# A streaming-encoder trunk on one core: odd tiles of frames normed and turned by a matrix product on TensorE, projected in pairs

## The chip, the cores and the metric

The kernel runs on one core of a Trainium2 chip. Its engines work beside each other, each through its own instructions in order: TensorE (PE, matrix products into the banks of PSUM), VectorE (DVE), ScalarE (ACT), GpSimd (POOL) and SyncE (SP), whose work here is to issue DMAs; ScalarE and GpSimd issue some too. Semaphores make one engine wait for another. The time is that of one execution on the device, in microseconds (us); of several executions the median counts.

## The reference

Batch 1, 2048 frames of 1024 channels, 16 learned frames ("meta tokens") ahead of them, depth 1. So the layer is an S5 mixer and a gated convolutional FFN, each behind an RMS norm and with a residual:

```python
hn = rms_norm(h, norm_mix)                       # h: meta tokens and x, 2064 x 1024
u = (hn @ s5_w_in).reshape(bsz, L, 64, 16)       # 64 groups of 16 channels
bu = einsum('gph,blgh->blgp', b_bar, u)          # complex, 64 states a group
s = scan(s[t] = a_bar * s[t - 1] + bu[t])        # complex, diagonal, over the frames
y = gelu(re(c s) + d_skip * u)
a, g = split(y @ s5_w_glu); h = h + a * sigmoid(g)
hn = rms_norm(h, norm_ffn)
h = h + (silu(conv(hn @ up_a)) * conv(hn @ up_b)) @ w_down
return h[:, 16:]
```

`a_bar` and `b_bar` come from `lam_re`, `lam_im`, `log_dt` and `b_re`, `b_im` (exponential, sine, cosine). All is float32.

## The kernel before

Matrix products with the large weights are made of three fp16 products (`mm3`, lines 76 to 78: high by high, high by low, low by high), so every operand is split into a high and a low fp16 part.

The first stage, which the change touches, projects the normed frames by `s5_w_in`. The 2048 frames are held as 16 tiles (`r` = 0 to 15) of 128 frames; a tile takes every sixteenth frame, and tile `r` holds frame 15 - r of each group of 16. The meta tokens are a tile of their own, `r = T = 16`. The order of the tiles is `seq` = 0, 1, 16, 2, 3, ... 15. A tile goes through these steps:

- `load_x` (L165): the tile, 512 KB, from HBM into a slot that the later stages will use for something else.
- `norm_a` (L171): sum of squares on ScalarE, then `rstd_of` on GpSimd (L70, L72).
- `norm_b` (L177, L178, L180): high part on ScalarE, low part on VectorE, both into `hl`, which has two slots that take turns; then two DMA transposes on SP's queue put them into `hnT[0]` and `hnT[1]`, with channels on the partitions.
- `emit_u(cb, q, part, w)` (L382): block `cb` of 128 channels of `u`, quad `q` (four tiles); `part` and `w` choose tiles in the quad. Eight steps of 128 input channels, three products each. The result fills a bank of PSUM.
- `evict_u` (L392): GpSimd puts a column of the meta tokens' result into `us` (L404), ScalarE the rest (L405), SP stores it to the DRAM tensor `ud` (L406). `load_u` (L412) reads it back as `U`, with another layout.

In this stage the blocks 0 to 2 are projected; their weights are loaded by `load_win`, scaled by the norm's gains and split by `split_win` (L352, L355, L357 for blocks 1 and 2; L354, L355, L357 for block 3). The blocks 3 to 7 follow in the next stage, the loop over `p`.

Beside it, `params()` is a generator whose steps (`next(par)`) compute `a_bar`, its powers `pre` and `pim` and the scan's coefficients `asc`: small operations on VectorE, `pow` on GpSimd (L245), a few transposes on TensorE. From them come the first block's matrices: `gen_b(0)` (L435 to L455, VectorE) and `transp(0)` (L465, L467) make `Win`, which turns `U` into states; `transp_c` (L473 to L476) and `gen_c(0)` (L487 to L493, VectorE) make `CA`, which turns states into outputs. `load_bc(0)` (L422, L425) loads their inputs in seven DMAs. `zero_kd` (L206, L208) and `load_cst` (L621) are small preparations for later stages.

The order is written out by hand: what a loop body emits, an engine runs in that order. `plan` says what is projected and evicted after which tile, `psteps` how many parameter steps are taken; quad 0 is projected tile by tile, quad 1 in halves, quads 2 and 3 whole. After the last tile come the rest of the quads, `transp_c`, `gen_b`, `drive(par)`, `gen_c`, `load_u(0)`, `transp(0)` and block 3's weights, mixed as `plan[15]` lists them. Then follow `emit_v(0)` (L534, L537: states from `Win` and `U`), `tcv` (L699) and its copies (L700, L701), and the loop over `p`, in which VectorE makes the next block's matrices and scans the states.

Of the kernel before, what the change touches and what calls it, by code (L numbers as in the profile page):

```python
# [11 lines left out]
F32 = mybir.dt.float32  # L12
# [3 lines left out]
P = 128  # L16
# [28 lines left out]
def tile_kernel(ctx: ExitStack, tc: tile.TileContext, x, meta, norm_mix, norm_ffn, w_in, lam_re, lam_im, log_dt,  # L45
# [95 lines left out]
    with ExitStack() as c2:  # L141
# [10 lines left out]
        def load_x(r, eng):  # L152

            if r == T:
                xt = s5.tile([P, D], F32, tag="tmp", name="xm")
            elif r < 3 or r >= 13:
                tag, bufs = (("S", 2), ("S", 2), ("Z", 1))[r if r < 3 else r - 13]
                xt = s5.tile([P, D], F32, tag=tag, bufs=bufs, name=f"xt{r}")
            else:
                if r % 2:  # L160
                    tag, bufs = (("Win", 1), ("CA", 2), ("CA", 2), ("U", 2), ("U", 2))[(r - 3) // 2]
                    xslots[r // 2] = s5.tile([P, 2, D], F32, tag=tag, bufs=bufs, name=f"xs{r}")
                xt = xslots[(r - 1) // 2 if r % 2 == 0 else r // 2][:, 1 - r % 2]
            n = P if r < T else T
            eng.dma_start(out=xt[:n], in_=x3[T - 1 - r] if r < T else meta)  # L165
            return xt

        def norm_a(r, xt):
            n = P if r < T else T
            ss = ld.tile([P, 1], F32, tag="ss", bufs=4, name=f"ss{r}")  # L170
            A.activation(junk[:n], xt[:n], AF.Square, accum_out=ss[:n])  # L171
            return rstd_of(ld, ss, n, f"a{r}")

        def norm_b(r, xt, rs):
            n = P if r < T else T
            hi, lo = hl[:n, r % 2, 0], hl[:n, r % 2, 1]
            A.activation(hi, xt[:n], AF.Copy, scale=rs[:n])  # L177
            V.scalar_tensor_tensor(lo, xt[:n], rs[:n], hi, op0=ALU.mult, op1=ALU.subtract)  # L178
            for t, s in zip(hnT if r < T else hmT, (hi, lo)):
                SY.dma_start_transpose(out=t[:, :, r, :] if r < T else t, in_=s)  # L180
# [21 lines left out]
            V.tensor_copy(gains[:, 8:16], tg[:, 8:16])  # L202

        def zero_kd():
            zero = ld.tile([P, 7 * T], F32, tag="zero", bufs=1, name="zero")
            V.memset(zero, 0.0)  # L206
            for i in range(2):
                SY.dma_start(out=kd[i].rearrange("h g x -> (h g) x")[:, 0:7 * T], in_=zero)  # L208
# [123 lines left out]
        def load_win(cb):  # L332
            if 0 < cb < 3:
                st = s5.tile([P, DK, P], F32, tag="wit", bufs=2, name=f"wst{cb}")
            else:
                st = ld.tile([P, DK, P], F32, tag="wst", bufs=1, name=f"wst{cb}")
            SY.dma_start(out=st, in_=wv[:, :, cb * P:(cb + 1) * P])
            return st

        def split_win(cb, st):  # L340
            wp = ld.tile([P, 2, DK, 16, 8], F16, tag="win", bufs=3, name=f"win{cb}")
            ws = [wp[:, i] for i in range(2)]
            src = st.rearrange("p dk (g h) -> p dk h g", h=16)
            if cb == 0:
                for dk in range(DK):
                    A.activation(ws[0][:, dk], src[:, dk], AF.Copy, scale=gains[:, dk:dk + 1])
                    V.scalar_tensor_tensor(ws[1][:, dk], src[:, dk], gains[:, dk:dk + 1], ws[0][:, dk], op0=ALU.mult,
                                           op1=ALU.subtract)
            else:
                for dk in range(DK):  # L350
                    if cb in (1, 2):
                        V.tensor_scalar(st[:, dk], st[:, dk], gains[:, dk:dk + 1], None, op0=ALU.mult)  # L352
                    else:
                        A.activation(st[:, dk], st[:, dk], AF.Copy, scale=gains[:, dk:dk + 1])  # L354
                A.copy(ws[0], src)  # L355
                yield
                V.tensor_tensor(ws[1], src, ws[0], op=ALU.subtract)  # L357
            yield
            wt[cb] = [t.rearrange("p dk h g -> p dk (h g)") for t in ws]
# [22 lines left out]
        def emit_u(cb, q, part=None, w=1, tag=0, dks=range(DK)):  # L382
            wh, wl = wt[cb]
            if (cb, q) not in ups:
                ups[cb, q] = psum.tile([P, 4, P], F32, tag=utags[tag], name=f"u{cb}_{q}")
            ps = ups[cb, q]
            r = slice(0, 4) if part is None else slice(part, part + w)
            rr = slice(4 * q + r.start, 4 * q + r.stop)
            for dk in dks:
                mm3(ps[:, r], wh[:, dk], wl[:, dk], hnT[0][:, dk, rr], hnT[1][:, dk, rr], dk == 0, dk == DK - 1)  # L390
# [26 lines left out]
        def load_bc(cb, eng=PO):  # L417
            gs = slice(G * cb, G * cb + G)
            xs = s5.tile([P, 2, G, T], F32, tag="X", name=f"X_{cb}")
            for i in range(2):  # L420
                for c, b in enumerate((b_re, b_im) if i == 0 else (b_im, b_re)):
                    eng.dma_start(out=xs[64 * c:64 * c + 64, i], in_=b[0, gs].rearrange("g p h -> p g h"))  # L422
            ct = s5.tile([P, 3, 64], F32, tag="ct", name=f"ct{cb}")
            for i, cc in enumerate((c_re, c_im, c_re)):
                eng.dma_start(out=ct[:, i], in_=cc[0, gs].rearrange("g h p -> (g h) p"))  # L425
            return xs, ct
# [182 lines left out]
        def drive(*gens):  # L609
            gens = list(gens)  # L610
            while gens:
                for g in list(gens):
                    if next(g, 0) == 0:
                        gens.remove(g)
# [15 lines left out]
        for r in seq[1:3]:  # L630
# [3 lines left out]
        ws[2] = load_win(2)  # L634
        xt[3] = load_x(3, SY)
        next(par)
        na[0] = norm_a(0, xt[0])
        setup(gst)
        plan = {0: "s", 1: "s", 2: "s", 3: "su", 5: ("h04", "h14", "h24"), 7: ("h06", "h16", "h26"), 8: ("e00", "e10"),
                9: ("e20",), 11: ("m022", "m123"), 12: ("e01", "e11", "e21", "m220"), 13: ("w",),  # L640
                14: (), 15: ("m031", "k", "b", "p", "c", "e02", "e12", "e22", "e03", "l", "m132", "t", "m233",
                              "x", "e13", "e23")}
        psteps = {**{i: 1 for i in range(0, 11)}, 11: 1, 12: 2, 13: 1, 14: 1, 15: 1, 16: 1}
        for i, r in enumerate(seq):
            if i == 0:
                norm_b(r, xt.pop(r), na.pop(r))
                drive(split_win(0, ws.pop(0)))
            for r2 in seq[i + 2:i + 3] if i else seq[1:3]:
                na[r2] = norm_a(r2, xt[r2])
            if i:  # L650
                norm_b(r, xt.pop(r), na.pop(r))
            if i + 5 < len(seq):
                xt[seq[i + 5]] = load_x(seq[i + 5], A)
            if 0 < i < 3:
                drive(split_win(i, ws.pop(i)))
            if r == 5:
                bc = load_bc(0, SY)
            if r == 6:
                zero_kd()
                load_cst()  # L660
            for _ in range(psteps.get(i, 0)):
                next(par, 0)
            for e in plan.get(r, ()):
                if e == "s":
                    for cb in range(min(3, r + 1)):
                        for part in range(r + 1) if r == cb else (r,):
                            emit_u(cb, 0, part=part, tag=cb)
                elif e == "u":
                    emit_u_meta([0, 1, 2])
                elif e[0] == "h":  # L670
                    for part in (int(e[2]) % 4,):
                        emit_u(int(e[1]), 1, part=part, w=2, tag=(3, 4, 0)[int(e[1])])
                elif e == "p":
                    drive(par)
                elif e == "b":
                    drive(gen_b(0, bc[0]))
                elif e == "k":
                    transp_c(0, bc[1])
                elif e == "c":
                    drive(gen_c(0))  # L680
                elif e == "t":
                    transp(0)
                elif e == "w":
                    ws[3] = load_win(3)
                elif e == "x":
                    drive(split_win(3, ws.pop(3)))
                elif e == "l":
                    load_u(0)
                elif e[0] == "m":
                    emit_u(int(e[1]), int(e[2]), tag=int(e[3]))  # L690
                else:
                    evict_u(int(e[1]), int(e[2]))
        quads = [(cb, q) for cb in range(3, NCB) for q in range(4)]
        takes = [3, 3, 3, 3, 4, 4, 0, 0]
        wn = 4
# [758 lines left out]
```

## Time and profile before

| | us |
|---|---|
| median of 3 executions | 2035.56 (2034.98 to 2037.89) |
| the profiled execution | 2040.73 |
| its span, first to last instruction | 2038.9 |
| TensorE busy | 1923.3 (94%) |
| VectorE busy | 1384.9 (68%) |
| ScalarE busy | 645.2 (32%) |
| GpSimd busy | 577.2 (28%) |

The page's busy shares are means over stages that differ. Times of single instructions are counted from the start of the span. The first stage ends, and the loop over `p` begins, near 139 us.

### The profile page before, as it was taken

The numbers are of one execution on the slowest core, as the hardware profiler recorded it, in microseconds if no ns is written. First come the engines' busy times: TensorE is split into PE (matmuls) and PEld (weight loads), VectorE is DVE, ScalarE is ACT, GpSimd is POOL, SyncE is SP. The second block draws the span as 40 slices with busy tenths as digits, with TensorE's granted clock in tenths as the row PEclk, the third lists the DMA queues.
The fourth block names the chain that finished last, engine by engine and source line by source line (L and its number), as shares of the span: only waits on it lengthen the run. The fifth ranks groups of instructions, "written<-read, shape, count | busy, mean of one in ns | idle before, by whom it ended". The sixth has DMA issues, their size and how long they took to land.

```text
span 2038.9 us, 28973 instructions
## 1 busy us (share of the span) xinstructions
PE 1923.3 (94%) x10992; PEld 957.5 (47%) x10992; DVE 1384.9 (68%) x1709; ACT 645.2 (32%) x1057; POOL 577.2 (28%) x644
## 2 busy tenths in 40 slices
PE   3699999689999999999999989999999999999999
PEld 3456666445444444444444434334444444444444
DVE  3489999944444348999999961345466666668982
ACT  5433423312222224544445441222222232322110
POOL 4221212400000014555555500366000001117630
PEclk9799999789999999999999999999999999999999
DMA  9967766958566656444444489999533333336443
GB/s 187 188 136 140 176 138 150 229 139 185 130 140 158 147 150 178 143 156 148 146 157 148 151 243 274 310 324 303 171 104 101 102 104 101 101 99 156 144 124 93
DMA packets 337223, 329.92 MB, mean 162 GB/s; under 512 B 150700, under 2 KB 238332, under 8 KB 337084
## 3 DMA queue, kind: packets, MB, share of 16 engines
q1 hardware_dynamic: 319164, 286.01, 52.9%
q0 software_dynamic: 8496, 27.30, 4.7%
q10 hardware_dynamic: 9424, 14.76, 2.9%
q8 instruction: 86, 1.41, 0.3%
q14 instruction: 53, 0.43, 0.1%
HBM read 183.82 MB, written 108.45 MB: 143 GB/s over the span
## 4 chain that ended last, share of the span: by engine, by line
PE 66%; DVE 8%; DMA 4%; issue 2%; ACT 1%; POOL 1%; SPq 1%; DVEq 0%; ACTq 0%; POOLq 0%
PE g L137 15%; PE p L78 11%; PE p L76 11%; PE p L77 11%; PE pq L76 3%; PE pq L77 3%; PE pq L78 3%; PE po L76 2%; PE po L77 2%; PE po L78 2%; DMA wc<-wcd 1%; DMA wcd<-wc 1%; DVE wc L914 1%; DVE y L1132 1%; DVE y L1131 1%
## 5 line engine op out<-in xcount | busy, mean ns | idle before, releaser
L76 PE MATMUL p<-hc,wc 128*128 128x512 f16 x1232 | 467.3, 379 | 2.3 <-DMA hc<-hl 1.7
L78 PE MATMUL p<-hc,wc 128*128 128x512 f16 x1232 | 467.5, 379 | 1.7 <-DVE wc L914 1.7
L77 PE MATMUL p<-hc,wc 128*128 128x512 f16 x1232 | 467.4, 379 | 0.9 <-DMA hc<-hl 0.9
L137 PE MATMUL g<-wg,yT 128*128 128x512 f16 x1536 | 334.3, 381 | 0.7 <-DMA yT<-yh 0.7
L914 DVE SCALAR_TENSOR_TENSOR wc<-fst,wc 128x512 f16<-128x512 f32 x209 | 184.7, 892 | 109.9 <-ACT wc L908 91.4
L137 PEld LDWEIGHTS <-yT 128*128 128x128 f16 x1536 | 150.2, 98 | 183.1 <-issue 2.6
L908 ACT ACTIVATE wc<-fst 128x512 f16<-128x512 f32 x209 | 125.9, 625 | 229.6 <-POOL fst L873 97.5
L78 PEld LDWEIGHTS <-wc 128*128 128x128 f16 x1232 | 120.2, 98 | 148.7 <-DVE wc L914 3.8
L76 PEld LDWEIGHTS <-wc 128*128 128x128 f16 x1232 | 120.1, 98 | 140.0 <-issue 1.8
L77 PEld LDWEIGHTS <-wc 128*128 128x128 f16 x1232 | 120.2, 98 | 138.9 <-DMA hc<-hl 1.2
L76 PE MATMUL pq<-wc,act 128*128 128x512 f16 x352 | 135.2, 384 | 16.6 <-DMA wc<-wcd 11.1
L76 PE MATMUL u<-hnT,win 128*128 128x512 f16 (+2 forms) x352 | 115.2, 337 | 25.6 <-DMA hnT<-hl 14.8
L77 PE MATMUL pq<-wc,act 128*128 128x512 f16 x352 | 135.1, 384 | 0.0
L78 PE MATMUL pq<-wc,act 128*128 128x512 f16 x352 | 134.8, 383 | 0.0
L77 PE MATMUL u<-hnT,win 128*128 128x512 f16 (+2 forms) x352 | 114.9, 337 | 16.9 <-DMA hnT<-hl 16.9
L76 PE MATMUL po<-wc,act 128*128 128x512 f16 x308 | 117.6, 382 | 3.4 <-DVE res L1292 3.4
L77 PE MATMUL po<-wc,act 128*128 128x512 f16 x308 | 117.6, 382 | 0.0
L78 PE MATMUL po<-wc,act 128*128 128x512 f16 x308 | 117.4, 381 | 0.0
L78 PE MATMUL u<-hnT,win 128*128 128x512 f16 (+2 forms) x352 | 115.0, 337 | 0.0
L1123 ACT ACTIVATE act<-hu,cwt 128x1024 f32<-128x1024 f32 x44 | 54.6, 1241 | 185.6 <-DVE hu L1224 141.3
L77 PEld LDWEIGHTS <-act 128*128 128x128 f16 x660 | 64.8, 98 | 99.1 <-issue 23.3
L1123 ACT ACTIVATE y<-hu,cwt 128x1024 f32<-128x1024 f32 x44 | 54.6, 1240 | 162.3 <-DVE hu L1224 123.2
(328 smaller groups left out, 2983.6 us busy)
## 6 DMA issues: line engine op xcount, KB each, us to landing
wc<-wcd SPq DMA_DIRECT2D x275, 256.0 KB, 2.7
wcd<-wc SPq DMA_DIRECT2D x253, 256.0 KB, 3.2
fst<-in_ffn_w_up_dram SPq DMA_DIRECT2D x44, 512.0 KB, 5.1
fst<-in_ffn_w_down_dram SPq DMA_DIRECT2D x44, 512.0 KB, 5.8
ud<-us SPq DMA_DIRECT2D x32, 258.0 KB, 5.3
U<-ud SPq DMA_DIRECT2D x16, 516.0 KB, 3.5
Toep<-kd SPq DMA_DIRECT2D x64, 128.0 KB, 5.4
yd<-yf POOLq DMA_DIRECT2D x8, 1024.0 KB, 7.6
```

What stands on the lines that cost most here:

```text
L76: PE.matmul(out=ps, lhsT=sh, rhs=mh, start=first, stop=False)
L77: PE.matmul(out=ps, lhsT=sh, rhs=ml, start=False, stop=False)
L78: PE.matmul(out=ps, lhsT=sl, rhs=mh, start=False, stop=last)
L137: PE.matmul(out=gps[t][o], lhsT=yT[t][:, a, dk], rhs=wg[b][:, dk, 512 * o:512 * o + 512], start=(dk == 0 and a + b == 0), stop=(dk == DK - ...
L908: A.activation(w[:, 0], src, AF.Copy, scale=GS)
L914: V.scalar_tensor_tensor(w[:, 1], src, GS, w[:, 0], op0=ALU.mult, op1=ALU.subtract)
L1123: A.activation(y, hu[:, 2:18], AF.Identity, bias=cwt[:, 3, c:c + 1], scale=cwt[:, 2, c:c + 1])
L1131: V.scalar_tensor_tensor(y, hu[:, 1:17], cwt[:, 1, c:c + 1], y, op0=ALU.mult, op1=ALU.add)
L1132: V.scalar_tensor_tensor(y, hu[:, 0:16], cwt[:, 0, c:c + 1], y, op0=ALU.mult, op1=ALU.add)
```

## The change

- Odd tiles (1, 3, ... 15) are no longer written to `hl` and transposed by DMA. `norm_t` makes a diagonal matrix `dg` of the tile's 128 norm factors on VectorE and multiplies the tile by it on TensorE, eight f32 products of 128 x 128 (`lhsT` the tile's 128 channels, `rhs` the diagonal): the result is normed and turned at once and lies in two banks of PSUM (`tag="v"`). `norm_c` copies it from there to `hnT`: the high part on ScalarE, the low part (a difference) on VectorE. Even tiles and the meta tokens go the old way, with `hl`'s slots counted by `hln`.
- The blocks 0 to 2 are projected for two tiles at a time (`part_u`, `w=2`), after each odd tile; each quad is evicted when its four tiles are done. `norm_a` runs three tiles ahead, `norm_t` and `norm_b` two, `norm_c` one, `load_x` six.
- `load_bc(0)` is issued before the first transpose. Parameter steps: one after tile 0, then two an iteration from the fourth on.
- `transp_c(0)`, `gen_b(0)`, `transp(0)`, block 3's weights and `gen_c(0)` come after the last tile, in that order, between the last three pieces of projection.
- `zero` uses the buffer of `dg` (`tag="dg"`, one buffer).

```diff
+        hln, turned = itertools.count(), {}
+
+        def norm_t(r, xt, rs):
+            dg = ld.tile([P, P], F32, tag="dg", bufs=1, name=f"dg{r}")
+            V.tensor_scalar(dg, ident, rs, None, op0=ALU.mult)
+            turned[r] = []
+            for h in range(2):
+                pt = psum.tile([P, 4, P], F32, tag="v", name=f"xT{r}_{h}")
+                for i in range(4):
+                    c = P * (4 * h + i)
+                    PE.matmul(out=pt[:, i], lhsT=xt[:, c:c + P], rhs=dg, start=True, stop=True)
+                turned[r].append(pt)
+
+        def norm_c(r):
+            for h, pt in enumerate(turned.pop(r)):
+                hi, lo = (t[:, 4 * h:4 * h + 4, r] for t in hnT)
+                A.copy(hi, pt)
+                V.tensor_tensor(lo, pt, hi, op=ALU.subtract)
+
         def norm_b(r, xt, rs):
             n = P if r < T else T
-            hi, lo = hl[:n, r % 2, 0], hl[:n, r % 2, 1]
+            k = next(hln) % 2
+            hi, lo = hl[:n, k, 0], hl[:n, k, 1]
             A.activation(hi, xt[:n], AF.Copy, scale=rs[:n])
             V.scalar_tensor_tensor(lo, xt[:n], rs[:n], hi, op0=ALU.mult, op1=ALU.subtract)
...
-            zero = ld.tile([P, 7 * T], F32, tag="zero", bufs=1, name="zero")
+            zero = ld.tile([P, 7 * T], F32, tag="dg", bufs=1, name="zero")
...
+        bc = load_bc(0, SY)
         na[0] = norm_a(0, xt[0])
         setup(gst)
-        plan = {0: "s", 1: "s", 2: "s", 3: "su", 5: ("h04", "h14", "h24"), 7: ("h06", "h16", "h26"), 8: ("e00", "e10"),
-                9: ("e20",), 11: ("m022", "m123"), 12: ("e01", "e11", "e21", "m220"), 13: ("w",),
-                14: (), 15: ("m031", "k", "b", "p", "c", "e02", "e12", "e22", "e03", "l", "m132", "t", "m233",
-                              "x", "e13", "e23")}
-        psteps = {**{i: 1 for i in range(0, 11)}, 11: 1, 12: 2, 13: 1, 14: 1, 15: 1, 16: 1}
+        norm_b(0, xt.pop(0), na.pop(0))
+        drive(split_win(0, ws.pop(0)))
+        for r in seq[1:3]:
+            na[r] = norm_a(r, xt[r])
+        norm_t(1, xt.pop(1), na.pop(1))
+        splits = [split_win(cb, ws.pop(cb)) for cb in (1, 2)]
+        for g in splits:
+            next(g)
+        for r in (4, 5):
+            xt[r] = load_x(r, A)
+
+        def part_u(q, p):
+            for cb in range(3):
+                emit_u(cb, q, part=p, w=2, tag=cb if q == 0 else (3, 0, 1)[cb])
+
+        def evicts(q):
+            for cb in range(3):
+                evict_u(cb, q)
+
         for i, r in enumerate(seq):
-            if i == 0:
-                norm_b(r, xt.pop(r), na.pop(r))
-                drive(split_win(0, ws.pop(0)))
-            for r2 in seq[i + 2:i + 3] if i else seq[1:3]:
-                na[r2] = norm_a(r2, xt[r2])
-            if i:
-                norm_b(r, xt.pop(r), na.pop(r))
-            if i + 5 < len(seq):
-                xt[seq[i + 5]] = load_x(seq[i + 5], A)
-            if 0 < i < 3:
-                drive(split_win(i, ws.pop(i)))
-            if r == 5:
-                bc = load_bc(0, SY)
-            if r == 6:
+            if i + 6 < T:
+                xt[i + 6] = load_x(i + 6, A)
+            if i + 3 < len(seq):
+                r3 = seq[i + 3]
+                na[r3] = norm_a(r3, xt[r3])
+            if i + 2 < len(seq):
+                r2 = seq[i + 2]
+                (norm_t if r2 % 2 else norm_b)(r2, xt.pop(r2), na.pop(r2))
+            if i + 1 < len(seq) and seq[i + 1] in turned:
+                norm_c(seq[i + 1])
+            if i < 2:
+                drive(splits[i])
+            for _ in range(1 if i == 0 else 2 if 3 <= i < 15 else 0):
+                next(par, 0)
+            if r == T:
                 zero_kd()
                 load_cst()
-            for _ in range(psteps.get(i, 0)):
-                next(par, 0)
-            for e in plan.get(r, ()):
...
+            elif r % 2:
+                if r % 4 == 1 and r > 1:
+                    evicts(r // 4 - 1)
+                if r < T - 1:
+                    part_u(r // 4, r % 4 - 1)
                 else:
+                    emit_u(0, 3, part=2, w=2, tag=3)
+            if r == 4:
+                emit_u_meta([0, 1, 2])
+            elif r == 13:
+                ws[3] = load_win(3)
+        transp_c(0, bc[1])
+        evict_u(0, 3)
+        load_u(0)
+        drive(gen_b(0, bc[0]))
+        emit_u(1, 3, part=2, w=2, tag=0)
+        transp(0)
+        emit_u(2, 3, part=2, w=2, tag=1)
+        evict_u(1, 3)
+        evict_u(2, 3)
+        drive(par)
+        drive(split_win(3, ws.pop(3)))
+        drive(gen_c(0))
         quads = [(cb, q) for cb in range(3, NCB) for q in range(4)]
         takes = [3, 3, 3, 3, 4, 4, 0, 0]
         wn = 4
```

Three places show the order of instructions. The first is VectorE while tiles 3 to 5 are prepared. Before, from the weights of block 2 on (the names behind the arrow are inputs; `xt` and `xs` are tiles of frames, `rsa` norm factors, `hl` the high and low halves):

```order
L352 TENSOR_SCALAR wst_144<-wst_144,gains 128x128 x8
L357 TENSOR_TENSOR win_336<-wst_144,win_336 128x1024
L178 SCALAR_TENSOR_TENSOR hl<-xt_142,rsa_224,hl 128x1024
L178 SCALAR_TENSOR_TENSOR hl<-xs_146,rsa_329,hl 128x1024
L178 SCALAR_TENSOR_TENSOR hl<-xs_146,rsa_353,hl 128x1024
L178 SCALAR_TENSOR_TENSOR hl<-xs_230,rsa_488,hl 128x1024
```

VectorE in the changed kernel, same place (`xT` is a turned tile in PSUM, `tl` the parameters turned by TensorE):

```order
L378 TENSOR_TENSOR win_223<-wst_144,win_223 128x1024
L179 TENSOR_SCALAR dg_349<-ident,rsa_260 128x128
L227 MEMSET zero 128x112
L199 SCALAR_TENSOR_TENSOR hl<-xs_146,rsa_347,hl 128x1024
L192 TENSOR_TENSOR hnT_93<-xT_0_351,hnT_92 128x4x128
L192 TENSOR_TENSOR hnT_93<-xT_1_356,hnT_92 128x4x128
L260 COPY lam<-tl 128x256
L179 TENSOR_SCALAR dg_403<-ident,rsa_375 128x128
```

The memset of `zero`, which stood eight tiles in, now stands between the diagonals of tiles 3 and 5, in their buffer.

The second is TensorE after the first pair of tiles in the changed kernel (`u_0` is quad 0 of a block, `win` a block's weights); before, no such rows exist and pieces of 128 columns follow each other:

```order
L78 MATMUL u_0_317<-hnT_92,win_223 128x256
L185 MATMUL xT_0_351<-dg_349,xs_146 128x128 x4
L185 MATMUL xT_1_356<-dg_349,xs_146 128x128 x4
L258 MATMUL tl<-ident,lst 128x64 x2
L258 MATMUL tl<-ident,zst 128x64 x2
L185 MATMUL xT_0_405<-dg_403,xs_234 128x128 x4
L185 MATMUL xT_1_410<-dg_403,xs_234 128x128 x4
L76 LDWEIGHTS win_172
```

Tiles 3 and 5 are both turned between the first and the second pair; later one turn stands ahead of each pair.

The third is ScalarE from the last tile to the first block's states `S`. Before (`cs` and `Win` are the first block's matrices, `wst` and `win` block 3's weights, `us` evicted projections):

```order
L475 ACTIVATE cs_1140<-pc_1137,sgn 128x128
L476 ACTIVATE cs_1140<-pc_1137 128x128
L405 ACTIVATE us_2_1211<-u_2_964 128x4x128
...
L467 COPY Win_1254<-wt_0_0_1255 128x512
...
L354 ACTIVATE wst_1086<-wst_1086,gains 128x128 x8
L355 CAST win_1304<-wst_1086 128x1024
L405 ACTIVATE us_3_1315<-u_3_1229 128x4x128
L405 ACTIVATE us_3_1315<-u_3_1279 128x4x128
L537 COPY S_1322<-vp_0_1323 128x512
```

And in the changed kernel:

```order
L191 CAST hnT_92<-xT_1_1169 128x4x128
L496 ACTIVATE cs_1293<-pc_1290,sgn 128x128
L497 ACTIVATE cs_1293<-pc_1290 128x128
L426 ACTIVATE us_3_1296<-u_3_1185 128x4x128
L488 COPY Win_1342<-wt_0_0_1343 128x512
...
L426 ACTIVATE us_3_1391<-u_3_1210 128x4x128
L426 ACTIVATE us_3_1391<-u_3_1235 128x4x128
L375 ACTIVATE wst_1260<-wst_1260,gains 128x128 x8
L376 CAST win_1398<-wst_1260 128x1024
L558 COPY S_1418<-vp_0_1419 128x512
```

Block 3's split moved behind the evictions of blocks 1 and 2; on VectorE, `gen_c(0)` moved from ahead of this split's difference to behind it:

```order
L378 TENSOR_TENSOR win_1398<-wst_1260,win_1398 128x1024
L508 TENSOR_TENSOR CA_1409<-pre,cs_1293 128x1088
L511 TENSOR_TENSOR ctm_0_1410<-pim,cs_1293 128x1088
L514 TENSOR_TENSOR CA_1409<-CA_1409,ctm_0_1410 128x1088
...
L728 TENSOR_SCALAR cwt<-tcv 128x132
```

Lines of the changed kernel are counted in its own file: up to `norm_a` they are those of before, up to the tile loop 21 more, behind the tile loop 28 more.

More of the change, by code (lines that the diff above doesn't have):

```diff
@@ L659, in tile_kernel @@
                 zero_kd()
                 load_cst()
-            for _ in range(psteps.get(i, 0)):
-                next(par, 0)
-            for e in plan.get(r, ()):
[L664 to L690, printed above, removed]
-                else:
-                    evict_u(int(e[1]), int(e[2]))
```

## The prediction

> **What bounds the kernel now.** I read the page first, then the first 140 us, because the diff ends where the loop over p begins. The windows view gives, for a stretch, the busy time of TensorE (PE), its weight loads, VectorE (DVE), ScalarE (ACT) and GpSimd (POOL), then TensorE's granted clock and the DMA share.
>
> ```profile
> span 2038.9 us, 28973 instructions
> 40.00:60.00 20.00, 14.41 (x265) 14.01 (x264) 4.02 (x4) 7.02 (x10) 11.94 (x18) 0.91 1.18 167
> 80.00:100.00 20.00, 10.43 (x61) 6.45 (x60) 11.35 (x40) 11.89 (x17) 3.08 (x9) 0.76 1.14 196
> 100.00:120.00 20.00, 19.94 (x97) 9.10 (x96) 16.07 (x24) 1.55 (x3) 2.53 (x4) 0.97 0.66 121
> 140.00:180.00 40.00, 36.85 (x300) 23.48 (x299) 39.04 (x53) 13.72 (x28) 6.61 (x11) 0.96 0.60 116
> ```
>
> So there are three stretches: up to 100 us no engine is full while the DMA share is about 1; at 100 to 120 TensorE is full; from 140 VectorE is full (39.04 of 40). The waits view says who holds the first one, and what VectorE waits for after 139 us.
>
> ```profile
> PE u L77 <- DMA hnT<-hl: 16.9, 6, 7.6
> PE u L76 <- DMA hnT<-hl: 14.8, 3, 9.8
> PE u L76 <- ACT us L405: 10.8, 3, 9.0
> ACT hl L177 <- DMA hnT<-hl: 35.1, 9, 8.8
> DVE cwt L700 <- PE tcv L699: 3.8, 1, 3.8
> hnT<-hl SPq DMA_TRANSPOSE x32, 8.5
> ```
>
> TensorE idles 32 us for turned tiles. ScalarE idles 35 us at the next tile's L177 until the transposes that still read `hl` have landed (median 8.5 us from issue); even the 10.8 us under "ACT us" are the same thing, since the eviction L405 stands behind such an L177. After 139 us VectorE's only long wait is 3.8 us for `tcv`, at the boundary itself. **So the marker is the start of L700 on VectorE: what moves it forward moves everything behind it**, because VectorE runs without a gap from there. In the rows of the timeline stand the start in us, the busy time, the engine, line and operation, and in brackets the idle time before and who ended it:
>
> ```profile
> 36.21 1.28 DVE L178 SCALAR_TENSOR_TENSOR hl<-xt,rsa,hl 128x1024 f16<-128x1024 f32 x1 [0.19 <-ACT hl L177]
> ...
> 105.55 1.28 DVE L178 SCALAR_TENSOR_TENSOR hl<-xt,rsa,hl 128x1024 f16<-128x1024 f32 x1 [2.52 <-ACT hl L177]
> ...
> 110.38 0.67 DVE L435 TENSOR_TENSOR tx<-X,coef 128x512 f32<-128x512 f32 x1
> ...
> 117.48 1.23 DVE L455 TENSOR_TENSOR wit<-wit,wtm 128x1024 f32<-128x1024 f32 x1
> ...
> 123.99 1.28 DVE L487 TENSOR_TENSOR CA<-pre,cs 128x1088 f32<-128x1088 f32 x1
> ...
> 130.23 1.29 DVE L493 TENSOR_TENSOR CA<-CA,ctm 128x1088 f32<-128x1088 f32 x1
> 133.22 1.89 DVE L357 TENSOR_TENSOR win<-wst,win 128x1024 f16<-128x1024 f32 x1 [1.70 <-ACT win L355]
> 138.94 0.30 DVE L700 TENSOR_SCALAR cwt<-tcv 128x132 f32<-128x132 f32 x1 [3.83 <-PE tcv L699]
> ```
>
> Tile 2 is normed at 36.21 and tile 15, thirteen tiles on, at 105.55: 5.33 us for a tile, 10.7 for a pair. Then `gen_b` (110.38 to 118.7, 8.3 us), parameters, `gen_c` (123.99 to 131.5, 7.5 us), the fourth weight split, and L700 at 138.94.
>
> **The prices of TensorE.** Start-to-start times, first with the clock at half, then at full:
>
> ```profile
> 43.00 0.22 PE L76 MATMUL u<-hnT,win 128*128 128x128 f16 x1 [3.81 <-DMA hnT<-hl]
> ...
> 44.04 0.31 PE L78 MATMUL u<-hnT,win 128*128 128x128 f16 x1
> 44.15 0.31 PE L76 MATMUL u<-hnT,win 128*128 128x128 f16 x1
> ...
> 53.99 0.22 PE L77 MATMUL u<-hnT,win 128*128 128x128 f16 x1
> 54.05 0.22 PE L78 MATMUL u<-hnT,win 128*128 128x128 f16 x1
> 125.85 1.04 PE L465 MATMUL wt<-ident,wit 128*128 128x128 f32 x8
> ...
> 176.79 0.39 PE L599 MATMUL yp<-Toep,U 128*128 128x128 f32 x2
> 177.01 0.60 PE L600 MATMUL yp<-CA,Z 128*128 128x256 f32 x2
> ```
>
> 128 columns cost 0.107 us at half clock (after an idle of 3.8 us) and 0.056 at full; the new 256-column pieces thus 0.214 and 0.107. A pair of tiles for three blocks is 3 x 8 x 3 = 72 of them, 7.7 us. The turn (L185 in the changed kernel) is an ordinary f32 matmul, which the trace does not show for L185; its nearest row is L599, also ordinary, f32 and 128 columns: two instructions, 0.22 us. Eight for a tile are 1.76 us, eight tiles 14 us. Ends: 0.11 each, as the f32 transposes of L465 take (eight begin within 0.76 us), and 0.44 at half clock; that is 7 us less or 14 more in all. I take 0.22. The Trainium skill, "Perfetto Trace Analysis", section Transposes, speaks against this part: a logical transpose should be issued as a transpose and not as a standard matmul. By it the same turn would cost 7 us and not 14; the trace agrees, L465 against L599 (0.11 to 0.22).
>
> **The change part by part.** *Removed:* 16 of 32 transposes and with them half of the waits for `hl`. A transposed tile is now wanted once a pair, and its cadence of 5.33 us is below the pair's 7.7 + 1.76 = 9.46 us on TensorE, so from the second pair on **TensorE sets the pace**. ScalarE's and VectorE's work for a pair lies under it:
>
> ```profile
> L177 ACT ACTIVATE hl<-xs,rsa 128x1024 f16<-128x1024 f32 x10 | 11.4, 1145 | 29.1 <-DMA hnT<-hl 29.1
> L171 ACT ACTIVATE junk<-xs 128x1024 f32<-128x1024 f32 x10 | 10.5, 1049 | 3.3 <-DMA ct<-in_s_c_re_dram 3.3
> ...
> L405 ACT ACTIVATE us<-u 128x512 f32<-128x512 f32 x12 | 6.4, 598 | 0.0
> ...
> L355 ACT CAST win<-wst 128x1024 f16<-128x1024 f32 x3 | 5.7, 1910 | 10.4 <-DVE wst L352 10.3
> ...
> L354 ACT ACTIVATE wst<-wst,gains 128x128 f32<-128x128 f32 x8 | 2.4, 389 | 0.0
> ...
> L467 ACT COPY Win<-wt 128x512 f32<-128x512 f32 x4 | 2.1, 588 | 4.7 <-PE wt L465 4.7
> ```
>
> ScalarE: two squares with their read-outs (2 x 1.25), one L177 (1.1), two copies out of PSUM (priced as L467, 2 x 0.59) and 1.5 evictions (0.9): 5.7 us. VectorE: L178 (1.28), two differences (between 0.6 and 1.3 each, half of an L178 and a whole one; I take 0.7, nearest to half) and the diagonal (0.3): 3 us, leaving 6 us a pair for the parameter steps, which ran in gaps before as well. POOL gets two `pow` steps an iteration for four iterations. The timeline's rows of POOL, then of SP's queue:
>
> ```profile
> 40.26 1.99 POOL L245 TENSOR_TENSOR q_mag<-q_ee,lam 128x4 f32<-128x4 f32 x2
> ...
> 58.28 0.75 SPq L422 DMA_DIRECT2D X<-in_s_b_re_dram  x1
> ...
> 63.64 4.00 SPq L180 DMA_TRANSPOSE hnT<-hl  x2
> ```
>
> The `pow` steps are 4 us beside 0.8 of rstd in an iteration of 4.7: just hidden; without cover each of four iterations slips 0.1 to 0.5 us.
>
> *Moved on SP's queue:* `load_bc(0)`, the two rows of SP above, now stands ahead of tile 0's transposes: seven issues, 58.28 to 63.64, 5.4 us. Their first issue slips from 11.0 to about 16.4; the second follows near 18, and with 8.5 us it lands at 26.6. On the other side, ScalarE's order (two casts at 1.9, a square, the meta tile, two copies) has tile 1 ready near 26. Pair 0 starts between 26 and 31; I take 27.5. It runs 16 pieces at half clock and 56 at full, 9.4 us: 36.9.
>
> *Added waits:* the turn of tile 3 (to 38.7) stands behind pair 0 on TensorE. The tile `zero` now shares the buffer of the diagonal `dg`, so VectorE's memset waits for that turn. Behind it on VectorE stand the low half of tile 4, tile 3's differences, `lam` and the diagonal of tile 5; on SP the stores of `zero`, four `cst` loads and tile 4's transposes. The store must land before tile 5's diagonal is written: about 42. TensorE then idles 3.3 us (ends: 0 and 6). Turn of tile 5, 43.8; pair 1, 51.5; the meta tokens' 72 matmuls of 16 columns, between 0 and 4 us by the 0.056 for 128, taken as 2: 53.5. Pairs 2 to 6 with a turn each, 5 x 9.46: 100.8. A third of pair 7 (block 0), 2.6: 103.4, and 0.6 for one part of a restart at half clock: **104**. By "TensorE: Matmul & The Clock Gate" of the Trainium skill, Part 1, the clock falls back after an idle window of about 3.4 us; the row at 43.00 agrees (3.81 us idle, then 0.107). By that rule the gap of 3.3 us would just pass, and the 0.6 would be 0, or 3.4 if the gap is longer.
>
> *The tail, in its new order.* Block 1's third, 2.6; sixteen transposes, 1.9 (`gen_b`, 8.3 us, ran before them on VectorE under pair 7's work); block 2's third, 2.6; its eviction, 0.6: 111.7. On ScalarE the fourth split stands behind that eviction: 2.4 + 1.9 = 116.0. On VectorE `gen_c` now stands behind the difference of this split (1.9): 117.9, and 7.5 for `gen_c`: 125.4. L700 follows at **126**. The other branch, block 0's store and reload, is shorter:
>
> ```profile
> 120.02 2.06 ACT L405 ACTIVATE us<-u 128x512 f32<-128x512 f32 x4
> ...
> 135.03 3.50 PE L534 MATMUL vp<-U,Win 128*64 128x128 f32 x60 [1.21 <-DMA U<-ud]
> ```
>
> Block 0's last eviction ended at 122.1 and L534 went on at 135.03, 13 us later; 3.9 more to L700. From 104.6 that makes 121.4, hidden by 4.6 us.
>
> **Sum.** L700 at 126 for 138.94: 13 us less. The profiled execution took 2040.73 us, of which 2038.9 are its span; the median of the three timed ones is 2035.56, 0.25% below. Taking the 13 from each gives 2027.7 and **2022.5**.
>
> **Rivals.**
> 1. *Start-up and the gap cost less.* Pair 0 at 26, no idle at 42, PSUM copies quick: 5 to 8 us more are gained, 2014.5 to 2017.5; with turns at 0.11 seven more. For it: the DMA share falls. Against: the 3.8 us gap row and L599's two instructions. Chance 0.14.
> 2. *The DMA keeps the old pace.* Loads of x stay as many and the share was 1.14; if a pair still takes 10.7 us, pairs 1 to 6 and the third end at 36.9 + 6 x 10.7 + 2 + 2.6 + 3.3 = 109 to 114 with a turn uncovered, L700 at 131 to 136: 2028 to 2033. Against: half the transposes are gone, and a transposed tile has two pairs' time to land. Chance 0.16.
> 3. *TensorE falls to half clock* (slower). If every pair has a gap like the one at 43.00, say since the copies of a turned tile release its two PSUM banks late, a pair costs 2 x 9.46. The point of balance is 13 us, 1.4 such pairs; three of them add 28 us: 2051. For it: the clock was 0.76 at 80 to 100 us. Against: those gaps came from `hl`, and a turn is issued a pair ahead of its use. Chance 0.07.
> 4. *The forecast*, 2017.5 to 2028: chance 0.63.
>
> The other side of no change begins at 0.2%, 4 us, about what a measurement of this kernel can tell. Below 2031.5 lie the forecast, rival 1 and a good half of rival 2: faster 0.86. The end of rival 2 and the mild end of rival 3, within 0.2%: 0.08. Slower: 0.06. The range leaves out the best part of rival 1, and on the other side the slow end of rivals 2 and 3: 2013 to 2031.
>
> **What would show it.** Right: L700 between 120 and 131 us; a pair of tiles every 9 to 10 us on TensorE with hardly an idle row between 55 and 105; L177's waits for `hnT` down to a few us; L185 as 128 instructions at 0.11 us each; VectorE idle before the fourth split's difference, then `gen_c`, then L700. Wrong: a granted clock under 0.9 at 60 to 100 us (rival 3), idle rows "DMA hnT" on TensorE (rival 2), L185 with 64 instructions, or L700 released by `tcv` after a late `U`. The forecast also falls if VectorE shows gaps after L700 that it did not have.

## The result, and the profile after

The changed kernel is slower. Beside runs of the kernel before on the same chip, its median is 2044.35 us against 2035.56 (nine runs each); the ratio is 1.0054, 95% interval 1.0037 to 1.0070. The forecast was 2022.5 us, with a range of 2013 to 2031. Executions that took over 1.5% longer than the fastest one of the same kernel, of which three of the cut kernels below have some, are left out of the medians.

The profiled execution took 2052.3 us, the longest of the nine. Its windows view, with the same columns as before, over the same stretches:

```profile
span 2050.5 us, 29214 instructions
40.00:60.00 20.00, 14.49 (x129) 13.37 (x127) 6.08 (x10) 6.74 (x11) 13.92 (x18) 0.83 0.67 142
80.00:100.00 20.00, 19.43 (x182) 17.56 (x180) 13.71 (x45) 9.24 (x15) 4.42 (x10) 1.00 0.43 94
100.00:120.00 20.00, 19.76 (x180) 17.82 (x179) 9.50 (x11) 5.44 (x11) 4.94 (x9) 1.00 0.40 102
140.00:180.00 40.00, 33.78 (x260) 22.40 (x258) 39.10 (x54) 11.52 (x25) 4.14 (x6) 0.91 0.54 108
```

In the middle of the first stage the picture is the forecast one: at 80 to 100 us TensorE is full (19.43 of 20) at full clock, and the DMA share has fallen from 1.14 to 0.43. The start is not: at 40 to 60 us TensorE is idle for a quarter of the time and the clock is 0.83. The waits of the first 130 us, and the timeline's rows of VectorE and TensorE at those places:

```profile
ACT hnT L191 <- PE xT L185: 15.9, 9, 7.8
...
DVE zero L227 <- PE xT L185: 8.1, 1, 8.1
...
PE u L77 <- DMA hnT<-hl: 7.5, 1, 7.5
...
PE xT L185 <- issue: 5.5, 1, 5.5
```

```profile
19.07 1.39 SPq L201 DMA_TRANSPOSE hnT<-hl  x1
...
31.28 0.39 PE L77 MATMUL u<-hnT,win 128*128 128x256 f16 x1 [7.52 <-DMA hnT<-hl]
...
40.61 1.95 PE L185 MATMUL xT<-dg,xs 128*128 128x128 f32 x16
...
42.66 0.15 DVE L227 MEMSET zero<- 128x112 f32 x1 [8.05 <-PE xT L185]
...
48.08 0.29 DVE L179 TENSOR_SCALAR dg<-ident,rsa 128x128 f32<-128x128 f32 x1 [2.59 <-DMA kd<-zero]
48.47 3.52 PE L185 MATMUL xT<-dg,xs 128*128 128x128 f32 x16 [5.51 <-issue]
...
113.61 0.38 PE L494 MATMUL pc<-ident,ct 128*128 128x128 f32 x2
...
126.44 1.92 DVE L378 TENSOR_TENSOR win<-wst,win 128x1024 f16<-128x1024 f32 x1 [13.54 <-ACT win L376]
...
135.74 0.29 DVE L728 TENSOR_SCALAR cwt<-tcv 128x132 f32<-128x132 f32 x1
```

The row of 31.28 is pair 0 getting tile 0's low half, 12.2 us after its transpose (19.07) was issued. The memset of `zero` waits 8.05 us for the turn of tile 3, the diagonal of tile 5 waits for the store of `zero`, and TensorE idles 5.51 us and then turns tile 5 at half clock (3.52 us in place of 1.95). L728, the marker, comes at 135.74, 3.2 us earlier than in the profile before. By the two profiles alone the first stage is then shorter, and the loss of 11.6 us (of the spans) would have to lie behind it. There is a candidate for that: between 355 and 400 us, where the loop over p ends and the gated unit's weights are loaded, the waits view has this row, for which the profile before shows 1.3 us:

```profile
PE mp L609 <- DMA Toep<-kd: 12.8, 1, 12.8
```

### The profile page after: what moved, and what is told of

The parts are those of the page before. It is cut to its first block, busy times and chain, and to the rows that moved or that the text cites. A ratio compares the mean times of both kernels' runs of the same rounds, so it can differ in the third digit from the quotient of the medians.

```text
span 2050.5 us, 29214 instructions
## 1 busy us (share of the span) xinstructions
PE 1935.4 (94%) x11120; PEld 982.1 (48%) x11120; DVE 1382.0 (67%) x1725; ACT 645.8 (31%) x1065; POOL 578.5 (28%) x644
## 4 chain that ended last, share of the span: by engine, by line
PE 74%; DVE 10%; DMA 7%; issue 5%; POOL 2%; ACT 1%; SPq 1%; DVEq 0%; ACTq 0%; POOLq 0%
PE g L137 15%; PE p L78 12%; PE p L76 12%; PE p L77 11%; PE pq L76 3%; PE pq L77 3%; PE pq L78 3%; PE po L76 2%; PE po L77 2%; PE po L78 2%; PE u L76 2%; DMA wc<-wcd 2%; PE u L77 2%; PE u L78 2%; DMA fst<-in_ffn_w_up_dram 1%
## 5 line engine op out<-in xcount | busy, mean ns | idle before, releaser
L76 PE MATMUL pq<-wc,act 128*128 128x512 f16 x352 | 135.0, 384 | 16.1 <-DMA wc<-wcd 10.7
L77 PE MATMUL u<-hnT,win 128*128 128x256 f16 (+1 forms) x352 | 114.2, 325 | 7.5 <-DMA hnT<-hl 7.5
L76 PE MATMUL u<-hnT,win 128*128 128x256 f16 (+1 forms) x352 | 114.5, 325 | 4.1 <-ACT hnT L191 4.1
L78 PE MATMUL u<-hnT,win 128*128 128x256 f16 (+1 forms) x352 | 114.1, 324 | 0.0
```

What stands on the lines that cost most here:

```text
L76: PE.matmul(out=ps, lhsT=sh, rhs=mh, start=first, stop=False)
L77: PE.matmul(out=ps, lhsT=sh, rhs=ml, start=False, stop=False)
L78: PE.matmul(out=ps, lhsT=sl, rhs=mh, start=False, stop=last)
```

## The experiments

Each group of runs stood beside runs of the kernel before on the same chip, whose medians were 2033.66, 2031.47, 2030.30 and 2030.92 us; so kernels of different groups are compared by their ratio to it.

### The late loss: a store in the way, or the step of the loop

SP's and GpSimd's rows of the changed kernel at that place:

```profile
355.35 0.57 POOL L96 DMA_DIRECT2D gst<-in_s_w_glu_dram  x1 [1.01 <-POOL wg L104]
...
357.78 5.46 SPq L128 DMA_TRANSPOSE yT<-yh  x2
...
361.97 1.20 POOL L627 DMA_DIRECT2D yd<-yf  x1
...
363.33 5.37 SPq L536 DMA_DIRECT2D kd<-ks  x4
377.02 5.12 SPq L543 DMA_DIRECT2D Toep<-kd  x8
```

The four small stores `kd<-ks` come behind a 1 MB store (`yd<-yf`), and the loads `Toep`, which wait for them, start at 377. Edit of the first two runs (`store_y` is the old store in a function; `hold` is set for the sixth block):

```diff
-            PO.dma_start(out=yd[...], in_=yf...)
+            held.append((cb, yf)) if hold else store_y(cb, yf, PO)
...
             uq(1)
+            if held:
+                store_y(*held.pop(), SY)
             load_toep(p)
```

In the changed kernel:

> The changed kernel; only the 1 MB store of the sixth block's output (L627) leaves GpSimd's queue and is issued from SyncE's, behind the four stores kd<-ks of the seventh block. Collision theory: the changed kernel loses its lead because these small stores now come onto the DMA engines together with the 1 MB store and the 512 KB loads gst; with the store out of the way the Toeplitz loads go from 377 back to about 370 us and TensorE's wait of 12.8 us for Toep falls under 3 us; the time falls by 6 to 9 us, to 2035 to 2038. Rival (the loss is somewhere else in what the change moved, and the late Toep is only its sign): Toep still at 375 or later or another wait in its place, 2042 to 2046.

In the kernel before:

> The same move of the 1 MB store made in the kernel before. Collision theory: there the stores kd<-ks were issued at 360.7 to 363.4 us, before the 1 MB store at 363.6, so there is little to gain: within 2 us of 2035.6. Rival (the store is in the way in both kernels alike): a gain of 5 us or more here too, and then it explains no difference between the two.

Measured: 2043.64 us, ratio 1.0053 (1.0031 to 1.0075), against 1.0054 without the edit; and 2033.65 us, ratio 1.0003 (0.9985 to 1.0021). In the profile of the edited changed kernel SP's rows of the timeline show the stores ahead of the 1 MB and `Toep` at 366, and the waits view has 3.4 us for it:

```profile
356.86 2.88 SPq L128 DMA_TRANSPOSE yT<-yh  x2
359.83 2.54 SPq L536 DMA_DIRECT2D kd<-ks  x4
362.42 0.59 SPq L635 DMA_DIRECT2D yd<-yf  x1
366.44 5.28 SPq L543 DMA_DIRECT2D Toep<-kd  x8
```

```profile
PE kp L525 <- DVE CA L514: 12.8, 2, 10.3
...
PE mp L609 <- DMA Toep<-kd: 3.4, 1, 3.4
```

The wait is nearly gone and the time is the same, so this wait is not the loss: the collision theory, the first one held, falls. In its place TensorE waits 10.3 us for VectorE's `CA` (2.7 us in the profile after, 6.6 in that of before). Nor does the wait of 12.8 us belong to the changed kernel as such: it was seen in the longest of nine executions, and the profile of the control further down, the same kernel unedited, has 4.5 us for it. The third run was to give L728 its old place:

```diff
         drive(gen_c(0))
+        for w in (D, D, 640):
+            V.tensor_tensor(junk[:, 0:w], junk[:, 0:w], junk[:, 0:w], op=ALU.subtract)
```

> The changed kernel with three idle subtractions on VectorE (1024, 1024 and 640 columns, about 3.2 us) ahead of L728, which puts the marker back to about 138.9 us, where the kernel before had it. Collision theory (the time hangs on how the loop over p and the loads at its end are in step): the boundary comes back to the pattern of before and the time falls to 2034 to 2038 although work is added. Rival (what the change altered is slow at the boundary whatever the step): 2044.4 plus 3.2, 2047 to 2049.

Measured: 2044.33 us, ratio 1.0061 (1.0041 to 1.0082). No return to 2034 to 2038. The 3.2 us do not show either, but six runs between 2039.4 and 2047.8 can't settle them. L728 stood at 144.0 in its profile and not at the 138.9 that was aimed at, so this run says little of the theory: 5 us of the lateness were not the delay's. That showed that the first stage itself differs from execution to execution.

### Where the loss lies: both kernels cut off

The profile of the edited kernel before has the marker (L708 there) 8.5 us earlier than the profile on which the prediction rests, with the same code up to that point:

```profile
130.48 0.29 DVE L708 TENSOR_SCALAR cwt<-tcv 128x132 f32<-128x132 f32 x1 [3.33 <-PE tcv L707]
```

So the first stage was timed by itself. Behind the copies of `tcv` (and, for the second pair, behind the sixth tile of the gated unit) stands:

```diff
+        SY.dma_start(out=o3[0][:, 0:176], in_=cwt.rearrange("p a b -> p (a b)"))
+        return
```

> The kernel before, cut off behind L700: everything after the first stage is left out. Its time is the marker plus some 6 us. First-stage theory (the profiled execution of before was a late one, L700 at 138.9, where another profile of the same code has 130.5): the median is nearer to the second, 137 to 141. Boundary theory (the first stage of the changed kernel is 3 us shorter and the loss comes at 375 to 450 us): 144 to 146.

> The changed kernel, cut off behind L728 in the same way. First-stage theory: 2 to 6 us longer than the cut kernel before, 141 to 146. Boundary theory: 3 us shorter than it.

> The kernel before, cut off inside the gated unit, behind the sixth of its sixteen tiles (about 530 to 550 us): what follows is left out. It gives the base for the next one.

> The changed kernel, cut off at the same tile. If the whole loss of 9 to 10 us stands ahead of this point: 8 to 11 us longer than the cut kernel before. Of it, by the first-stage theory as much as the first pair of cuts shows (2 to 6); by the boundary theory all of it and 3 us more come between the two cuts. If it is under 3 us longer, the loss comes in the last 1500 us.

Measured medians: 132.9 us (132.3 to 134.1, four runs) and 141.7 (141.4 to 143.0, three) for the first cut, **8.8 us more**; 568.7 (564.2 to 571.4, five) and 577.5 (576.0 to 580.4, four) for the second, 8.8 more too; with all executions counted, 10.2 and 8.5 more. The whole kernel lost 8.8. So the loss is in the first stage. Both expectations had missed its size: 137 to 141 us were expected of the cut kernel before, and 2 to 6 us more of the changed one. The timeline of the cut kernel before, tiles 2 and 15 on VectorE and the marker:

```profile
33.64 1.28 DVE L178 SCALAR_TENSOR_TENSOR hl<-xt,rsa,hl 128x1024 f16<-128x1024 f32 x1 [0.20 <-ACT hl L177]
...
97.13 1.28 DVE L178 SCALAR_TENSOR_TENSOR hl<-xt,rsa,hl 128x1024 f16<-128x1024 f32 x1 [2.23 <-ACT hl L177]
129.62 0.30 DVE L700 TENSOR_SCALAR cwt<-tcv 128x132 f32<-128x132 f32 x1 [2.37 <-PE tcv L699]
```

and of the cut changed kernel, pair 0, tile 5's turn and the marker:

```profile
31.91 0.40 PE L77 MATMUL u<-hnT,win 128*128 128x256 f16 x1 [7.99 <-DMA hnT<-hl]
...
50.69 3.49 PE L185 MATMUL xT<-dg,xs 128*128 128x128 f32 x16 [6.35 <-issue]
...
137.88 0.29 DVE L728 TENSOR_SCALAR cwt<-tcv 128x132 f32<-128x132 f32 x1
```

Thirteen tiles take 63.5 us, 4.88 a tile, **9.77 a pair**, where the profile on record had 10.7; the same two rows give 9.7 in the profile of the kernel cut at the second place and 9.9 in that of e2. That is the pace at which TensorE runs the pairs of the changed kernel (its turns stand 9.7 us apart, at one place 10.8). Between the pairs there was nothing to gain.

### The parts of the loss

One edit each, of the changed kernel. The zero tile in another buffer:

```diff
-            zero = ld.tile([P, 7 * T], F32, tag="dg", bufs=1, name="zero")
+            zero = s5.tile([P, 4, P + 1], F32, tag="us", bufs=2, name="zero")[:, 0, 0:7 * T]
```

> The changed kernel with the zero tile in a buffer of the evictions (us) in place of the diagonal's. Theory on the first stage: VectorE's waits of 8.05 us (memset) and 2.59 us (diagonal of tile 5) go, TensorE's idle 5.5 us ahead of tile 5's turn goes with its half clock (another 1.5 to 3 us), and L728 comes at 128 to 131 us instead of 135.7. Rival: the transposes or x tiles are late anyway, L728 at 134 to 136. The end: by the collision theory it is not 2044 minus 6 but depends on the new step, anywhere between 2030 and 2046; if a gain at L728 is simply carried to the end, 2037 to 2039.

`load_bc(0)` behind tile 0's transposes:

```diff
-        bc = load_bc(0, SY)
         na[0] = norm_a(0, xt[0])
         setup(gst)
         norm_b(0, xt.pop(0), na.pop(0))
+        bc = load_bc(0, SY)
```

> The changed kernel with the seven loads of load_bc(0) put back behind tile 0's transposes on SyncE's queue. Start-up theory (the 5.4 us that these issues take delay tile 0's turned halves, and so pair 0): tile 0's transposes at 11 to 14 us in place of 17.6 to 19.1, pair 0 on TensorE at 25 to 28 in place of 31 to 35, L728 at 132 to 134, the time 4 to 6 us under the changed kernel's 2044.4. Rival (tile 1's hand-made turn or the x loads hold pair 0 anyway): pair 0 at 30 or later, no gain.

`gen_c` ahead of the split:

```diff
+        drive(gen_c(0))
         drive(split_win(3, ws.pop(3)))
-        drive(gen_c(0))
```

> The changed kernel with gen_c ahead of the split alone. Tail theory: L728 at 130 to 132 in place of 136 to 139, 6 to 7 us under the changed kernel: 2037 to 2038. Rival as above: 2042 or more.

The first two together, and all three:

> Both: the zero tile in a buffer of the evictions, and load_bc(0) behind tile 0's transposes. If the two terms are separate they add up: L728 at 126 to 129 us, 2033 to 2035, level with the kernel before. Rival (both are the same wait seen twice, the DMA engines being full up to 60 us): no better than the zero tile alone, 2037 to 2038.

> The same two and gen_c ahead of the fourth block's split on VectorE, which in the changed kernel idles 13.5 us ahead of that split's difference (L378). Tail theory: gen_c's 7.5 us go into that gap, then the difference, then L728, now released by tcv: L728 6 to 7 us earlier than in the kernel with two edits, at 119 to 122 us; 2026 to 2029, faster than both kernels. Rival (U's store and reload, or the weights' split on ScalarE, holds TensorE's tcv): 2 us or less from this edit.

The changed kernel once more, as a control:

> The changed kernel again, unaltered, beside the others. If the loss stands as in the first comparison: ratio to before 1.004 to 1.007, and L728 in its profile at 135 to 139 us, where three of four profiles of the code before have 129 to 130.5.

Measured, with three places of each profile's timeline (pair 0 is the last wait ahead of its run of products):

| kernel | median, us | ratio to before (95%) | pair 0 | turn of tile 5 | L728 |
|---|---|---|---|---|---|
| changed, first group | 2044.35 | 1.0054 (1.0037 to 1.0070) | 31.28 | 48.47 | 135.74 |
| changed, control | 2050.28 | 1.0099 (1.0076 to 1.0123) | 35.10 | 53.81 | 141.58 |
| zero tile | 2037.40 | 1.0031 (1.0010 to 1.0052) | 30.80 | 44.16 | 131.58 |
| load_bc | 2033.10 | 1.0021 (1.0003 to 1.0039) | 24.52 | 42.86 | 130.59 |
| gen_c | 2034.75 | 1.0027 (1.0015 to 1.0039) | 32.97 | 51.14 | 131.23 |
| zero tile, load_bc | 2031.68 | 1.0009 (0.9994 to 1.0024) | 24.66 | 37.84 | 125.29 |
| all three | 2023.92 | 0.9973 (0.9959 to 0.9986) | 24.46 | 38.91 | 117.26 |

By L728, where the parts can be read without the rest of the kernel: `zero` gives 5.3 us (130.59 to 125.29), `load_bc` 6.3 (131.58 to 125.29), `gen_c` 8.0 (125.29 to 117.26); 19.6 together. Each figure is the difference of two single executions, and five profiles with the unedited first stage have L728 anywhere from 135.74 to 141.58. Most of that spread lies ahead of pair 0: counted from pair 0, L728 follows after 104.3 to 106.5 us in these five, after 106.1 with `load_bc` moved, 100.8 with `zero` moved and 98.3 with `gen_c` moved, so that the last two stand clear of it. By the medians `zero` and `load_bc` together, and `gen_c` on top of them, are clear gains; the intervals of the three single edits overlap that of the first group, and no unedited changed kernel ran in their groups. In one part each, theory and rival were told apart: pair 0 follows `load_bc`, the gap ahead of tile 5's turn follows `zero`, the tail follows `gen_c`. The row that shows the last one, in the kernel with all three:

```profile
109.65 1.29 DVE L514 TENSOR_TENSOR CA<-CA,ctm 128x1088 f32<-128x1088 f32 x1
115.42 1.91 DVE L378 TENSOR_TENSOR win<-wst,win 128x1024 f16<-128x1024 f32 x1 [4.49 <-ACT win L376]
117.26 0.27 DVE L728 TENSOR_SCALAR cwt<-tcv 128x132 f32<-128x132 f32 x1
```

`gen_c` stands in what were VectorE's 13.5 us of idle time ahead of L378, and the marker follows the split at once.

The control's loss is twice that of the first group, and the two intervals do not meet. Its profile shows where: pair 0 at 35.10, 3.8 us later, while from pair 0 to the marker it takes 106.5 us against 104.5. With `load_bc` moved back, pair 0 starts at 24.5 to 24.7 in all three profiles. What it waits for there is no longer a transpose but tile 1's low half on VectorE, as in the profile with this edit alone:

```profile
24.52 0.37 PE L77 MATMUL u<-hnT,win 128*128 128x256 f16 x1 [1.07 <-DVE hnT L192]
```

### The price of the turn, and what is lost behind the marker

With all three edits, the sixth block's store moved as above (e9), the turn made as transposes (e10), or both (e11):

```diff
-            dg = ld.tile([P, P], F32, tag="dg", bufs=1, name=f"dg{r}")
-            V.tensor_scalar(dg, ident, rs, None, op0=ALU.mult)
+            V.tensor_scalar(xt, xt, rs, None, op0=ALU.mult)
...
-                    PE.matmul(out=pt[:, i], lhsT=xt[:, c:c + P], rhs=dg, start=True, stop=True)
+                    PE.transpose(out=pt[:, i], in_=xt[:, c:c + P], identity=ident)
```

> The kernel with the three edits (zero tile, load_bc, gen_c) and with the sixth block's 1 MB store on SyncE's queue behind kd<-ks. Collision theory (part of the lead of 12 us at L728 is lost at 340 to 380 us to that store): 4 to 6 us under the three-edit kernel, ratio to before 0.994 to 0.996. Rival (the lead ends at the loads of the gated unit's weights, or is lost now and then only): within 2 us of it, ratio 0.996 to 0.998.

> The three-edit kernel with the turn made as transposes: VectorE scales the tile in place (128x1024 f32, under 1.3 us) in place of writing the diagonal, and TensorE turns it with the identity. Price theory: a turn falls from 1.95 us to about 1.0, a pair from 9.7 to 8.8 us, L728 from 117 to 110 or 112; the end gains as much or, if the lead is lost at the boundary, less. Rival (the pace of a pair is set by the transposes through the DMA or by ScalarE): the pair stays at 9.7.

> All of it together. If both theories hold: ratio to before 0.990 to 0.993; if neither, 0.997.

Measured: 2021.43 us, ratio 0.9957 (0.9940 to 0.9974); 2020.12 us, 0.9953 (0.9937 to 0.9969); 2019.41 us, 0.9951 (0.9934 to 0.9968). All three beat both kernels; among themselves, and against the three-edit kernel's 0.9973 (0.9959 to 0.9986), the intervals overlap, so neither edit's gain at the end is shown; for e11, 0.9951 lies between what was expected if both theories hold and if neither does. What the turn costs is:

```profile
59.19 1.06 PE L184 MATMUL xT<-ident,xs 128*128 128x128 f32 x8
...
114.80 0.29 DVE L727 TENSOR_SCALAR cwt<-tcv 128x132 f32<-128x132 f32 x1 [1.56 <-PE tcv L726]
```

Half of the 1.95 us, with eight instructions in place of sixteen. The pairs follow: the turn after this one begins at 67.95, 8.8 us on, where the three-edit kernel has 9.7, so the rival (a pair stays at 9.7) falls, and TensorE sets the pace. The marker gains 2.5 us on the three-edit kernel (117.26) and 3.2 on e9's profile (118.00), not the 5 to 7 expected; 1.56 us of the difference are a wait for `tcv` that the three-edit kernel's row of 117.26 does not have.

## Why the prediction was wrong, point by point

**The marker of before, 138.94.** The first step that failed is "Sum. L700 at 126 for 138.94". The 138.94 was read correctly, but of an execution that was late there: the three other profiles of the same code have 128.95, 129.62 and 130.48, and the cut kernel's median puts the marker near 127.9 (132.9 less the 5.0 that its profiled execution, 134.61, took beyond the marker). The prediction saw that the profiled execution took 0.25% more than the median, and carried its 13 us over to the median all the same. So 8.5 to 11 of the 13 us were the lateness of that execution, with its 10.7 us a pair against 9.7 to 9.9. Against a usual marker the forecast of 126 is a gain of 2 to 4.5 us. With the 9.7 us by which the changed kernel's marker missed 126 (the next points), this makes 18 to 21 of the 21.8 us between forecast and median.

**Pair 0, 27.5.** Mis-sized: it starts at 31.3 to 35.1. The issue times were near (16.4 and 18 forecast, 17.6 and 19.1 measured). The 8.5 us for a transpose, a median over the whole stage, were not: tile 0's low half took 12 to 16 us. The runs with `load_bc` moved back settle that this move is the cause: 24.5 to 24.7.

**The gap ahead of tile 5's turn, 3.3 us.** The mechanism was right (`zero` in the buffer of `dg`), the size not: 5.5 to 6.4 us in the profiles of the changed kernel, with the turn at half clock behind it (3.5 us for 1.95; the pieces of pair 1 that follow, 0.11 us each, are at full clock again). From pair 0 to this turn the forecast had 14.5 us; the profile after has 17.2.

**The pace of 9.46 a pair.** Nearly right: 9.7, at one place 10.8, with a turn of 1.95 where 1.76 was forecast. From tile 5's turn (42.0, forecast) to the end of the pairs (104) it had 62 us; to L494, which follows them, the profile has 65.1. The Trainium skill, "Perfetto Trace Analysis", section Transposes, spoke against this part of the change; e10 agrees with it, 1.06 us for 1.95.

**The tail, 22 us.** Right: 113.61 to 135.74 is 22.1. That the order of this tail was itself a loss was in the prediction's working (`gen_c` behind the split's difference), but not compared: from L473 at 111.30 to the marker the cut kernel before takes 18.3 us, and with `gen_c` moved the changed kernel takes 14.7.

```profile
111.30 0.38 PE L473 MATMUL pc<-ident,ct 128*128 128x128 f32 x2
```

The three misses make up the marker: 3.8 (pair 0), 2.7 (to the turn of tile 5), 3.1 (half clock, turns and the one long step), 9.6 of the 9.7 us between 126 and 135.74. So the first sign that the prediction named, L700 between 120 and 131, failed.

**The U branch hidden; the gain carried to the end.** The first held (L728 has no wait for `tcv`). The second held for the loss in the first group: 8.8 us at the first cut, at the second and in the medians. Of the control's 19.4 us, though, its marker (141.58 against some 129.6) accounts for 12; where the other 7 arose is open. For a large lead it is not shown: the three-edit kernel is 12 us ahead at the marker of what the kernel before usually has, and 5.5 us (0.27%) ahead at the end. In a single execution the marker does not settle the end at all: what lies behind it took from 1898 us (e1) to 1919 (the three-edit kernel, in the longest of its twelve executions) in the profiles; why is open.

**The rivals.** Rival 2's time at the marker (131 to 136) is what the profile shows, but not for its reason: the DMA share fell and the pairs kept their own pace. Rival 3, the slower one, did not happen: the clock is 1.00 at 80 to 120 us. The mechanism that made the kernel slower, two delays at the start and a worse order at the tail, in a stage where the new pace gains nothing, was none of the rivals.

## What to carry to other kernels

The first stage, whose pace was set by DMAs, differed by 10 us between executions of the same code; before a gain is computed against one profile, see whether that execution was a usual one, and do the sum against the stage's own pace. A step moved ahead of the first transfers of a pipeline delays everything behind it: the seven loads took 6.9 us to issue there (10.56 to 17.49 on SP), and pair 0 came 6 to 10.6 us later for it. A shared buffer and the order of two steps at the tail cost 13.3 us at the marker, more than the 12 us by which the mended kernel leads there: with both mended and the loads put back, the same idea is 0.27% faster than the kernel before.

## What the runs showed of the hardware

- The same first stage took 129 to 139 us to the marker in four profiles; the median from issue to landing of its 32 transposes was 8.5 us in the longest and 4.8 in that of the first cut. What slowed them there was not found.
- SP's issue of two transposes took 5.46 us where GpSimd's 512 KB load had been issued 2.4 us ahead of them (rows of 355.35 and 357.78), and 2.88 in the profile of e1 (row of 356.86), where such a load had been issued 0.3 us ahead (356.56). Which load in flight makes the difference was not tried.
- An idle time of 1.58 us ahead of tile 5's turn was followed by half clock in the profile of the kernel with the zero tile and `load_bc` mended, and in that with the zero tile alone (a turn of 3.44 us):

```profile
37.84 3.57 PE L185 MATMUL xT<-dg,xs 128*128 128x128 f32 x16 [1.58 <-issue]
```

and by full clock in that of the kernel with all three edits, and in e9's (2.02 us):

```profile
38.91 2.02 PE L185 MATMUL xT<-dg,xs 128*128 128x128 f32 x16 [1.58 <-issue]
```

So the clock's fall hangs on more than the length of the gap ahead of the instruction, and the prediction's "would just pass" for a gap of 3.3 us was not safe.
